# Low halves of ff1's weights made by an accumulating transfer, and q's products one step earlier on VectorE

## The chip, the cores and the metric

The program runs on one core of a Trainium2 chip. Its time is the device time in microseconds (us) of one execution, the median of several. The core's engines work side by side, each through its own list of instructions in order: TensorE (PE, with its weight loads as PEld), VectorE (DVE), ScalarE (ACT), GpSimd (POOL) and SyncE (SP, which here only issues transfers). They wait for each other through semaphores. 16 DMA engines move data between the memory outside the core (HBM) and SBUF.

## The reference, cut to what matters

One layer over 256 tokens of 1024 channels: a token mixer of three groups behind one input projection (1024 to 3072) and one output projection, then an MLP.

```
h = rms_norm(x, norm_mix);  z = h @ w_in                       # 12 column chunks of 256
qs = silu(q);  k = (1 - lb) * sigmoid(-f)                      # HGRN2 group, decays from f
y = concat(rms_norm(griffin), hgrn2, rms_norm(attention));  x = x + y @ w_out
h = rms_norm(x, norm_mlp)
u = square(relu(h @ w_ff1))                                    # 1024 -> 4096
x = x + u @ w_ff2                                              # 4096 -> 1024
return rms_norm(x, norm_final)
```

All data are float32. The products run on TensorE in the type fp32r, which holds fewer bits, so each operand is split into a high part (rounded to fp32r) and a low part (the value less its high part), and each product is the sum of three: high x high, high x low, low x high.

## The kernel before

All weights come in 48 chunks of 1 MB, each a tile of 128 x 2048: 12 of `w_in` (0 to 11), 4 of `w_out` (12 to 15), then `w_ff1[0]`, `w_ff1[1]` (16, 17), and from there `w_ff2` and `w_ff1` by turns: 18 is `w_ff2[0]`, 19 is `w_ff1[2]`, 20 is `w_ff2[1]`, 21 is `w_ff1[3]`, and so on to 45, `w_ff1[15]`, and 46 and 47, the last two of `w_ff2`. SP loads chunk i into one of three `raw` buffers (L94). `split_w` (L96) then makes two halves of it: ACT writes the high half into `wh` (L71, a cast), DVE subtracts it from `raw` into `wl` (L72). When both halves are done, chunk i + 3 is loaded into the buffer that has come free. `wh` and `wl` have four buffers each.

The order of the work is written out by hand. The first 84 slots are groups of TensorE products (input projection, output projection, the first chunk of ff1); a table `plan` says which other steps are issued ahead of each slot. Slot 17 belongs to chunk 4. Ahead of it stands `hg_dqk` (L377), which on TensorE multiplies `qk`, the product of q and k that DVE makes in `hg_q_dve` (L370 to L372). In row 13 of the table the order was: `hg_f_fd` (ACT), the second half of chunk 4's split, `hg_q_dve`.

After the slots a loop runs over the 16 chunks j of `w_ff2`. In each turn TensorE does `ff2_mm` with chunk j (24 products of 512 columns) and then `ff1` for chunk j + 2 (48 products of 256 columns: for each 128 x 128 block, `x1h` and `x1l` with `wh`, `x1h` with `wl`; L301, L302, L303). Between them ACT and DVE split two chunks that come two steps later: one of `w_ff2`, one of `w_ff1`. Then `ff1_out` (L772) takes ff1's result: ACT does the ReLU (`fr`, L778) and its square rounded (`uh`, L779), DVE the exact square and its low part (`fu`, `ul`, L780 and L781). Ahead of the loop stands `x1_ss` (L817), two squares with sums of 128 x 1024 on ACT.

Of the kernel before, what the change touches and what calls it, by code (L numbers as in the profile page):

```python
# [8 lines left out]
F32 = mybir.dt.float32  # L9
F32R = mybir.dt.float32r  # L10
I32 = mybir.dt.int32
AF = mybir.ActivationFunctionType
OP = mybir.AluOpType
AX = mybir.AxisListType

P = 128
S = 256
D = 1024
KT = D // P
# [13 lines left out]
def trunk_kernel(ctx: ExitStack, tc, x, x_t, w_in, w_out, w_ff1, w_ff2, small, hg_norm, norm_final, out):  # L33
    nc = tc.nc
    V, A, G, T = nc.vector, nc.scalar, nc.gpsimd, nc.tensor

    const = ctx.enter_context(tc.tile_pool(name="const", bufs=1))
    RAW = 3
    raw_p = ctx.enter_context(tc.tile_pool(name="raw", bufs=RAW))
    spl_p = ctx.enter_context(tc.tile_pool(name="spl", bufs=4))  # L40
# [20 lines left out]
    def free(name):  # L61
        idle.extend(held.pop(name))

    def wt(name, shape, tag=None, bufs=None, dt=F32):
        return work.tile(shape, dt, name=name, tag=tag or name, bufs=bufs)

    def flat(t):
        return t.rearrange("p a b -> p (a b)")

    def split(hi, lo, src):  # L70
        A.copy(hi, src)  # L71
        V.tensor_tensor(lo, src, hi.bitcast(F32), op=OP.subtract)  # L72
# [4 lines left out]
    NI = len(in_order)  # L77
    IG, IX, IY = 2, 3, 4
    NF = 16
    chunks = [w_in[c] for c, _ in in_order] + [w_out[j] for j in range(4)]  # L80
# [4 lines left out]
            chunks.append(w_ff1[j + 2])  # L85
    NCH = len(chunks)
    raw, hi_w, lo_w = {}, {}, {}

    def load(i, n=1):
        if i < NCH:  # L90
            raw[i] = raw_p.tile([P, 2048], F32, name=f"raw{i}", tag="raw")
            for h in range(n):
                s_ = slice(h * 2048 // n, (h + 1) * 2048 // n)
                nc.sync.dma_start(raw[i][:, s_], chunks[i][:, s_])  # L94

    def split_w(i, h, n=2):  # L96
        if i < NCH:
            if h == 0:
                hi_w[i] = spl_p.tile([P, 2048], F32R, name=f"wh{i}", tag="wh")
                lo_w[i] = spl_p.tile([P, 2048], F32R, name=f"wl{i}", tag="wl")  # L100
            s_ = slice(h * 2048 // n, (h + 1) * 2048 // n)
            split(hi_w[i][:, s_], lo_w[i][:, s_], raw[i][:, s_])
            if h == n - 1:
                load(i + RAW)
# [194 lines left out]
    def mm3(o, l, r, first, last):  # L299
        (lh, ll), (rh, rl) = l, r  # L300
        T.matmul(o, lh, rh, start=first, stop=False)  # L301
        T.matmul(o, lh, rl, start=False, stop=False)  # L302
        T.matmul(o, ll, rh, start=False, stop=last)  # L303
# [27 lines left out]
    yTl = wt("yTl", [P, KT, S], dt=F32R)  # L331
# [399 lines left out]
    x1h = wt("x1h", [P, KT, S], tag="hTh", dt=F32R)  # L731
    x1l = wt("x1l", [P, KT, S], tag="hTl", dt=F32R)
# [29 lines left out]

    FI = NI + 4
    uh, ul = {}, {}

    def ff1_mm(o, i, c, k):
        wh = hi_w[i].rearrange("p (k c) -> p k c", c=CW)
        wl = lo_w[i].rearrange("p (k c) -> p k c", c=CW)
        cs = slice(c * 128, (c + 1) * 128)
        mm3(o, (wh[:, k, cs], wl[:, k, cs]), (x1h[:, k, :], x1l[:, k, :]), k == 0, k == KT - 1)  # L770

    def ff1_evac(j, parts):  # L772
        r = wt("fr", [P, 512], tag="sc", bufs=3)
        u = wt("fu", [P, 512], tag="pr", bufs=2)
        uh[j] = wt("uh", [P, 512], tag="PT", bufs=8, dt=F32R)
        ul[j] = wt("ul", [P, 512], tag="PT", bufs=8, dt=F32R)
        for src, s_ in parts:
            A.activation(r[:, s_], src, AF.Relu)  # L778
            A.activation(uh[j][:, s_], r[:, s_], AF.Square)  # L779
            V.tensor_tensor(u[:, s_], r[:, s_], r[:, s_], op=OP.mult)  # L780
            V.tensor_tensor(ul[j][:, s_], u[:, s_], uh[j][:, s_].bitcast(F32), op=OP.subtract)  # L781
# [3 lines left out]
    def ff1(j, i):  # L785
        ps = ff1_ps[j] = mis(f"f{j}")
        for c in range(2):
            for k in range(KT):
                ff1_mm(ps[:, c * 256:(c + 1) * 256], i, c, k)

    def ff1_out(j):
        ff1_evac(j, [(ff1_ps[j], slice(0, 512))])
        free(f"f{j}")
# [3 lines left out]
    def ff2_mm(j, i, kk, t, n):  # L797
        if j == 0 and kk == 0:
            facc[t, n] = mis(f"fo{t}{n}")
        cs = slice(kk * 256 + t * 128, kk * 256 + (t + 1) * 128)  # L800
        big_mm(facc[t, n], uh[j][:, cs], ul[j][:, cs], i, kk, n, j == 0 and kk == 0,
               (t, n) == (1, 1) and j == NF - 3 and kk == 1)
# [3 lines left out]
    def ff1_first(c, kg):  # L806
        if kg == 0:
            f0[c] = mis(f"f0{c}")[:, 0:256]
        for k in range(4 * kg, 4 * kg + 4):
            ff1_mm(f0[c], FI, c, k)  # L810
# [6 lines left out]
    def x1_ss():  # L817
        for t in range(2):
            A.activation(sq2, xt[:, t, :], AF.Square, accum_out=ss2[:, 0, t:t + 1])
        V.tensor_scalar(ss2[:, 0, :], ss2[:, 0, :], 1.0 / D, EPS, op0=OP.mult, op1=OP.add)  # L820
        V.reciprocal(r2, ss2[:, 0, :])
# [3 lines left out]
    S_ = split_w  # L825
# [16 lines left out]
        10: [(x_bc,), (x_rb,), (hg_f_ev,), (hg_q_ev,), (S_, 3, 0), (S_, 3, 1)],  # L842
        11: [(hg_f_act,), (hg_f_kb,), (S_, 4, 0)],
        12: [(hg_q_act,)],
        13: [(hg_f_fd,), (S_, 4, 1), (hg_q_dve,)],
        14: [(hg_qd,), (S_, 5, 0)],
        15: [(S_, 6, 0)],
        16: [(S_, 6, 1)],
# [56 lines left out]
    S_(FI + 2, 0)  # L905
    S_(FI + 2, 1)
    ff1(1, FI + 1)
    S_(FI + 3, 0)
    S_(FI + 3, 1)
    ff1_out(1)  # L910
    x1_ss()
    nc.sync.dma_start(nfb, bass.AP(tensor=norm_final.tensor, offset=norm_final.offset, ap=[[0, P], [1, D]]))
    i = FI + 2
    tnt = sorted(tn)
    tail = {}
    for j in range(NF):
        if j < NF - 2:
            for kk in range(2):
                for t, n in tnt:
                    ff2_mm(j, i, kk, t, n)  # L920
        else:
            tail[j] = i
        split_w(i + 2, 0)
        split_w(i + 2, 1)
        i += 1
        if j + 2 < NF:
            ff1(j + 2, i)
            split_w(i + 2, 0)
            split_w(i + 2, 1)
            ff1_out(j + 2)  # L930
            i += 1

# [131 lines left out]
```

## Time and profile before

| | before |
|---|---|
| median of 3 runs | 322.01 us (321.96 to 323.01) |
| the profiled execution's own time | 322.01 us |
| its span, first to last instruction | 320.3 us |
| TensorE busy | 309.7 us (97%) |
| VectorE busy | 192.1 us (60%) |
| ScalarE busy | 171.9 us (54%) |
| GpSimd busy | 32.7 us (10%) |
| DMA | 55.71 MB, mean 174 GB/s |

The 1.7 us between the span and the execution's own time lie outside the instructions. Busy shares are means over the whole span; the MLP loop takes the stretch from about 143 us to 302 us. Times below are counted from the start of the span.

### The profile page before, as it was taken

To read this page: it belongs to the slowest core of one execution; us is meant where nothing else is said; L and a number is where in the kernel's file an instruction comes from. 1 tells how busy PE (TensorE), PEld (TensorE's weight loads), DVE (VectorE), ACT (ScalarE), POOL (GpSimd) and SP (SyncE) were. 2 spreads that over 40 slices of the span, in tenths; PEclk is the share of its full clock that TensorE was granted. 3 is DMA by queue.
4 is the path that set the end of the run, shared out by engine and by line. 5 is a ranking of instruction groups with operands and counts; after the bars stand their busy time and mean duration, and the time that the engine had idled before them with its cause. 6 is when DMAs were issued, how large, how long until landed. Compare 5 with 4: busy or idle time off the path is not lost.

```text
span 320.3 us, 5290 instructions
## 1 busy us (share of the span) xinstructions
PE 309.7 (97%) x2164; PEld 283.8 (89%) x2164; DVE 192.1 (60%) x287; ACT 171.9 (54%) x283; POOL 32.7 (10%) x83
## 2 busy tenths in 40 slices
PE   7999899999999999999999999999999999999991
PEld 6999799998999888998899899889989988988881
DVE  1847999994545494598635733753663474375353
ACT  3869499683675370687623642562463265256132
POOL 8338400011502000000000000000000000000000
PEclk9999999999999999999999999999999999999999
DMA  7995463352037336048665256336425624630003
GB/s 198 412 405 209 140 257 131 133 171 93 2 97 298 132 132 264 0 152 327 251 256 217 89 220 263 115 149 262 186 93 249 256 80 191 262 131 3 0 4 129
DMA packets 9961, 55.71 MB, mean 174 GB/s; under 512 B 1232, under 2 KB 1488, under 8 KB 4048
## 3 DMA queue, kind: packets, MB, share of 16 engines
q1 hardware_dynamic: 9216, 54.06, 44.8%
q10 hardware_dynamic: 720, 1.31, 1.3%
q8 instruction: 17, 0.28, 0.3%
q14 instruction: 8, 0.07, 0.1%
HBM read 54.32 MB, written 1.05 MB: 173 GB/s over the span
## 4 chain that ended last, share of the span: by engine, by line
PE 89%; ACT 3%; DVE 2%; DMA 2%; issue 2%; POOLq 0%; POOL 0%; DVEq 0%; ACTq 0%
PE banks L301 27%; PE banks L303 27%; PE banks L302 26%; PE banks L405 2%; DMA raw<-in_w_in_dram 2%; ACT wh L71 1%; PE banks L641 1%; PE banks L659 1%; PE banks L168 1%; PE banks L675 1%; PE banks L676 1%; PE banks L458 1%; PE banks L521 1%; PE banks L674 1%; DVE wl L72 0%
## 5 line engine op out<-in xcount | busy, mean ns | idle before, releaser
L72 DVE TENSOR_TENSOR wl<-raw,wh 128x1024 fp32r<-128x1024 f32 (+1 forms) x100 | 113.6, 1182 | 20.7 <-ACT wh L71 19.0
L71 ACT CAST wh<-raw 128x1024 fp32r<-128x1024 f32 (+1 forms) x100 | 95.4, 1009 | 3.6 <-DMA raw<-in_w_in_dram 3.6
L301 PE MATMUL banks<-x1h,wh 128*128 128x256 f32 x256 | 72.6, 283 | 0.0
L302 PE MATMUL banks<-x1l,wh 128*128 128x256 f32 x256 | 72.5, 283 | 0.0
L303 PE MATMUL banks<-x1h,wl 128*128 128x256 f32 x256 | 72.5, 283 | 0.0
L778 ACT ACTIVATE fr<-banks 128x512 f32<-128x512 f32 (+1 forms) x17 | 9.7, 573 | 87.2 <-PE banks L303 87.2
L780 DVE TENSOR_TENSOR fu<-fr 128x512 f32<-128x512 f32 (+1 forms) x17 | 11.2, 660 | 69.5 <-ACT fr L778 69.5
L303 PE MATMUL banks<-wh,ul 128*128 128x512 f32 (+1 forms) x132 | 51.5, 390 | 0.1
L301 PE MATMUL banks<-wh,uh 128*128 128x512 f32 (+1 forms) x132 | 51.5, 390 | 0.0
L302 PE MATMUL banks<-wl,uh 128*128 128x512 f32 (+1 forms) x132 | 51.5, 390 | 0.0
L301 PEld LDWEIGHTS banks<-x1h,wh 128*128 128x128 f32 x256 | 49.0, 192 | 0.7
L302 PEld LDWEIGHTS banks<-x1l,wh 128*128 128x128 f32 x256 | 49.0, 191 | 0.6
L303 PEld LDWEIGHTS banks<-x1h,wl 128*128 128x128 f32 x256 | 49.1, 192 | 0.0
L301 PE MATMUL banks<-hTh,wh 128*128 128x256 f32 x128 | 37.6, 294 | 0.5 <-ACT hTh L161 0.5
L302 PE MATMUL banks<-hTl,wh 128*128 128x256 f32 x128 | 36.5, 285 | 0.8 <-DVE hTl L162 0.8
L303 PE MATMUL banks<-hTh,wl 128*128 128x256 f32 x128 | 36.3, 284 | 0.0
L303 PEld LDWEIGHTS banks<-wh,ul 128*128 128x128 f32 x132 | 24.9, 189 | 6.1 <-DVE ul L781 0.6
L301 PEld LDWEIGHTS banks<-wh,uh 128*128 128x128 f32 x132 | 25.0, 189 | 5.3 <-ACT uh L779 0.4
L302 PEld LDWEIGHTS banks<-wl,uh 128*128 128x128 f32 x132 | 24.9, 189 | 5.0
L302 PEld LDWEIGHTS banks<-hTl,wh 128*128 128x128 f32 x128 | 24.5, 192 | 1.3 <-DVE hTl L162 1.2
L301 PEld LDWEIGHTS banks<-hTh,wh 128*128 128x128 f32 x128 | 24.5, 191 | 1.2 <-ACT hTh L161 0.7
L303 PEld LDWEIGHTS banks<-hTh,wl 128*128 128x128 f32 x128 | 24.5, 192 | 0.1
(198 smaller groups left out, 412.5 us busy)
## 6 DMA issues: line engine op xcount, KB each, us to landing
raw<-in_w_ff_dram SPq DMA_DIRECT2D x32, 1024.0 KB, 5.0
raw<-in_w_in_dram SPq DMA_DIRECT2D x10, 1024.0 KB, 5.6
raw<-in_w_out_dram SPq DMA_DIRECT2D x4, 1024.0 KB, 4.9
raw<-in_w_in_dram ACTq DMA_DIRECT2D x4, 256.0 KB, 7.3
xtok<-in_x_dram SPq DMA_DIRECT2D x2, 512.0 KB, 7.9
xa<-in_x_dram SPq DMA_DIRECT2D x2, 512.0 KB, 6.7
xa<-in_x_t_dram SPq DMA_DIRECT2D x3, 256.0 KB, 6.2
raw<-in_w_in_dram SPq DMA_DIRECT2D x2, 256.0 KB, 8.1
```

What stands on the lines that cost most here:

```text
L71: A.copy(hi, src)
L72: V.tensor_tensor(lo, src, hi.bitcast(F32), op=OP.subtract)
L168: T.transpose(pair[n % 2][:, i * 256 + t * 128:i * 256 + (t + 1) * 128], src[:, t, (k0 + n) * P:(k0 + n + 1) * P], ident)
L301: T.matmul(o, lh, rh, start=first, stop=False)
L302: T.matmul(o, lh, rl, start=False, stop=False)
L303: T.matmul(o, ll, rh, start=False, stop=last)
L405: T.matmul(ps[:, par, g * 64:(g + 1) * 64], kB[r, hp, hs], rhs, start=True, stop=True)
L458: T.matmul(dst, att_d[:, (hp * 2 + half) * 2 + par, :], bv[:, half, h * 64:h * 64 + 64], start=True, stop=(half == 0))
L521: T.matmul(ps[:, c * 256:(c + 1) * 256], spw[:, wofs + c * 128:wofs + (c + 1) * 128], xc[:, c, :], start=True, stop=True)
L641: T.matmul(ps_s[2 * pair + par][:, os], q[r, c, qs], k[r, c, ks], start=True, stop=True)
L778: A.activation(r[:, s_], src, AF.Relu)
L780: V.tensor_tensor(u[:, s_], r[:, s_], r[:, s_], op=OP.mult)
```

## The change

There are two edits.

First, the 14 chunks `w_ff1[2]` to `w_ff1[15]` (the odd chunk numbers 19 to 45, the set `neg`) are split in another way. ACT writes the negative rounded value, -round(w), into the low tile (two instructions of 128 x 1024) and again into the high tile (two more). Then POOL issues a transfer that reads the same 1 MB chunk from HBM once more and adds it to the low tile in place, so that the low tile holds w - round(w) as before. DVE has no part in it. The high tile is now negative, so the activations it meets are too: `x1_neg` makes `nxh` = -`x1h` and turns `x1l` into -`x1l` (four ACT instructions of 128 x 1024, once, after `ff1_out(1)`). The products are then the same three.

Second, in row 13 of the table `hg_q_dve` goes ahead of `hg_f_fd` and of the second half of chunk 4's split.

```diff
+    neg = set(range(NI + 7, NCH - 2, 2))
...
+    nxh = wt("nxh", [P, KT, S], tag="yTl", dt=F32R)
+
+    def split_n(i):
+        if i in neg:
+            hi_w[i] = spl_p.tile([P, 2048], F32R, name=f"wh{i}", tag="wh")
+            lo_w[i] = spl_p.tile([P, 2048], F32R, name=f"wl{i}", tag="wl")
+            for o in (lo_w[i], hi_w[i]):
+                for s_ in (slice(0, 1024), slice(1024, 2048)):
+                    A.activation(o[:, s_], raw[i][:, s_], AF.Copy, scale=-1.0)
+            nc.gpsimd.dma_start(lo_w[i], chunks[i], accum_op=OP.add)
+            load(i + RAW)
+        else:
+            split_w(i, 0)
+            split_w(i, 1)
+
+    def x1_neg():
+        for s_ in (slice(0, 4), slice(4, 8)):
+            A.activation(flat(nxh[:, s_, :]), flat(x1h[:, s_, :]).bitcast(F32), AF.Copy, scale=-1.0)
+            A.activation(flat(x1l[:, s_, :]), flat(x1l[:, s_, :]).bitcast(F32), AF.Copy, scale=-1.0)
...
-        mm3(o, (wh[:, k, cs], wl[:, k, cs]), (x1h[:, k, :], x1l[:, k, :]), k == 0, k == KT - 1)
+        T.matmul(o, wh[:, k, cs], (nxh if i in neg else x1h)[:, k, :], start=k == 0, stop=False)
+        T.matmul(o, wh[:, k, cs], x1l[:, k, :], start=False, stop=False)
+        T.matmul(o, wl[:, k, cs], x1h[:, k, :], start=False, stop=k == KT - 1)
...
-        13: [(hg_f_fd,), (S_, 4, 1), (hg_q_dve,)],
+        13: [(hg_q_dve,), (hg_f_fd,), (S_, 4, 1)],
...
-    S_(FI + 3, 0)
-    S_(FI + 3, 1)
+    split_n(FI + 3)
     ff1_out(1)
+    x1_neg()
     x1_ss()
...
             ff1(j + 2, i)
-            split_w(i + 2, 0)
-            split_w(i + 2, 1)
+            split_n(i + 2)
             ff1_out(j + 2)
```

On DVE, around chunk 4 of the input projection (`wl_461` and `wl_462` are its low tile, `qc` and `qk` are q's products), before:

```order
L360 TENSOR_SCALAR kB<-kB,omlb 128x256 x2
L72 TENSOR_TENSOR wl_461<-raw_348,wh_460 128x1024 x2
L371 TENSOR_TENSOR qc<-qc,qk 128x512
L372 TENSOR_TENSOR qk<-qc,kB 128x512
L375 TENSOR_TENSOR qd<-qc,fd 128x512
L72 TENSOR_TENSOR wl_511<-raw_368,wh_510 128x1024
```

and in the changed kernel:

```order
L361 TENSOR_SCALAR kB<-kB,omlb 128x256 x2
L72 TENSOR_TENSOR wl_462<-raw_349,wh_461 128x1024
L372 TENSOR_TENSOR qc<-qc,qk 128x512
L373 TENSOR_TENSOR qk<-qc,kB 128x512
L72 TENSOR_TENSOR wl_462<-raw_349,wh_461 128x1024
L376 TENSOR_TENSOR qd<-qc,fd 128x512
L72 TENSOR_TENSOR wl_512<-raw_369,wh_511 128x1024
```

The two products have moved ahead of the second half of chunk 4's low part; `qd` stays behind it.

On ACT, from the split of chunks 18 and 19 to that of chunk 21, at the start of the MLP loop (tiles 1600, 1656, 1701, 1757 are chunks 18 to 21), before:

```order
L71 CAST wh_1600<-raw_1438 128x1024 x2
L71 CAST wh_1656<-raw_1458 128x1024 x2
L778 ACTIVATE fr<-banks 128x512
L779 ACTIVATE uh<-fr 128x512
L819 ACTIVATE sq_208,ss_209<-xa 128x1024 x2
L71 CAST wh_1701<-raw_1574 128x1024 x2
L71 CAST wh_1757<-raw_1606 128x1024 x2
L778 ACTIVATE fr<-banks 128x512
```

and in the changed kernel:

```order
L71 CAST wh_1601<-raw_1439 128x1024 x2
L774 ACTIVATE wl_1658<-raw_1459 128x1024 x2
L774 ACTIVATE wh_1657<-raw_1459 128x1024 x2
L800 ACTIVATE fr<-banks 128x512
L801 ACTIVATE uh<-fr 128x512
L783 ACTIVATE nxh<-x1h 128x1024
L784 ACTIVATE x1l<-x1l 128x1024
L783 ACTIVATE nxh<-x1h 128x1024
L784 ACTIVATE x1l<-x1l 128x1024
L841 ACTIVATE sq_208,ss_209<-xa 128x1024 x2
L71 CAST wh_1707<-raw_1575 128x1024 x2
L774 ACTIVATE wl_1764<-raw_1607 128x1024 x2
```

Eight instructions of 128 x 1024 now stand where two casts stood between chunk 18's split and `x1_ss`. On POOL, whose list had ended here but for the last two powers, 14 transfers have come in; the first three and what stands ahead of them:

```order
L153 TENSOR_TENSOR hrr<-hrv,nhalf 128x8
L153 TENSOR_TENSOR crr<-crv,nhalf 128x2
L775 DMA wl_1658<-in_w_ff_dram 128x2048
L775 DMA wl_1764<-in_w_ff_dram 128x2048
L775 DMA wl_1861<-in_w_ff_dram 128x2048
```

Each waits for ACT's two writes of its low tile. DVE's list has lost 28 subtractions of 128 x 1024.

## Rows read from the trace of the kernel before

**Rows 1.** The page, part 1: busy us (share of the span) and instructions.
```profile
PE 309.7 (97%) x2164; PEld 283.8 (89%) x2164; DVE 192.1 (60%) x287; ACT 171.9 (54%) x283; POOL 32.7 (10%) x83
```

**Rows 2.** PE's waits, two of four: line, waited for: us in total, times, longest.
```profile
PE banks L146 <- POOL ident masks.py:199: 1.4, 1, 1.4
PE banks L380 <- DVE qk L372: 1.2, 1, 1.2
```

**Rows 3.** Timeline of PE at slot 17: start, us, instruction [idle before <-releaser].
```profile
32.95 0.28 PE L302 MATMUL banks<-hTl,wh 128*128 128x256 f32 x1
33.07 0.28 PE L303 MATMUL banks<-hTh,wl 128*128 128x256 f32 x1
34.59 1.10 PE L380 MATMUL banks<-bones,qk 128*128 128x64 f32 x8 [1.24 <-DVE qk L372]
```

**Rows 4.** Timeline of DVE there.
```profile
31.43 1.46 DVE L72 TENSOR_TENSOR wl<-raw,wh 128x1024 fp32r<-128x1024 f32 x1 [1.23 <-ACT wh L71]
32.81 0.99 DVE L371 TENSOR_TENSOR qc<-qc,qk 128x512 f32<-128x512 f32 x1
33.84 0.69 DVE L372 TENSOR_TENSOR qk<-qc,kB 128x512 f32<-128x512 f32 x1
34.45 0.99 DVE L375 TENSOR_TENSOR qd<-qc,fd 128x512 f32<-128x512 f32 x1
```

**Rows 5.** Timeline of ACT there.
```profile
28.85 0.63 ACT L368 ACTIVATE qk<-qc 128x512 f32<-128x512 f32 x1
...
30.37 4.82 ACT L71 CAST wh<-raw 128x1024 fp32r<-128x1024 f32 x5
```

**Rows 6.** Busy time by stretch: us, PE PEld DVE ACT POOL (x), PEclk, DMA share, GB/s.
```profile
245.05:256.40 11.35, 11.35 (x74) 10.26 (x73) 6.02 (x6) 5.02 (x6) 0.00 (x0) 1.00 0.47 186
250.65:256.40 5.75, 5.75 (x49) 5.73 (x48) 1.47 (x2) 0.00 (x0) 0.00 (x0) 1.00 0.92 363
142.80:154.20 11.40, 11.40 (x75) 10.31 (x74) 7.76 (x10) 7.30 (x10) 0.00 (x0) 1.00 0.78 297
32.00:72.00 40.00, 38.74 (x354) 37.02 (x353) 38.73 (x72) 31.71 (x55) 4.40 (x5) 1.00 0.47 166
```

**Rows 7.** Timeline of ACT in one later turn of the loop.
```profile
245.25 0.60 ACT L778 ACTIVATE fr<-banks 128x512 f32<-128x512 f32 x1 [6.31 <-PE banks L303]
...
246.42 3.89 ACT L71 CAST wh<-raw 128x1024 fp32r<-128x1024 f32 x4
```

**Rows 8.** Timeline of PE at the starts of ff1(2), ff1(3) and a later ff1.
```profile
148.43 0.28 PE L301 MATMUL banks<-x1h,wh 128*128 128x256 f32 x1
...
148.66 0.28 PE L303 MATMUL banks<-x1h,wl 128*128 128x256 f32 x1
...
160.02 0.28 PE L303 MATMUL banks<-x1h,wl 128*128 128x256 f32 x1
...
262.26 0.28 PE L303 MATMUL banks<-x1h,wl 128*128 128x256 f32 x1
```

**Rows 9.** Timeline of ACT at the start of the loop.
```profile
137.99 3.88 ACT L71 CAST wh<-raw 128x1024 fp32r<-128x1024 f32 x4
143.01 0.60 ACT L778 ACTIVATE fr<-banks 128x512 f32<-128x512 f32 x1 [1.14 <-PE banks L303]
143.64 0.63 ACT L779 ACTIVATE uh<-fr 128x512 fp32r<-128x512 f32 x1
144.18 1.05 ACT L819 ACTIVATE sq<-xa 128x1024 f32<-128x1024 f32 x1
...
146.40 3.97 ACT L71 CAST wh<-raw 128x1024 fp32r<-128x1024 f32 x4
```

**Rows 10.** The page, part 6: DMA issues, KB each, median us to landing.
```profile
raw<-in_w_ff_dram SPq DMA_DIRECT2D x32, 1024.0 KB, 5.0
```

**Rows 11.** DMA issues from 142 to 159 us, same columns.
```profile
raw<-in_w_ff_dram SPq DMA_DIRECT2D x5, 1024.0 KB, 6.5
```

**Rows 12.** Timeline of SP's issues in that stretch.
```profile
142.06 2.60 SPq L94 DMA_DIRECT2D raw<-in_w_ff_dram  x2
```

## The prediction

> **What bounds the kernel now.** I read the busy shares first: TensorE is busy for 309.7 of 320.3 us [rows 1]. Then its waits: there are four lines of them, and the two longest, 1.4 us for the identity at the very start and 1.2 us for `qk` at L380, are the only ones of over a microsecond [rows 2]. Then the stretches: in a turn of the MLP loop TensorE is busy for all of 11.35 us, beside 6.02 us of DVE, 5.02 us of ACT and a DMA share of 0.47 [rows 6]. So the reader is to see two things. Work taken off DVE in the loop shortens nothing by itself, since nothing there waits for DVE. And the only wait in the middle that the change can take away is that at L380.
>
> **q's products (gain).** TensorE starts its last product ahead of L380 at 33.07, would go on 0.12 later (its step from 32.95 to 33.07), and starts L380 at 34.59 [rows 3]: 34.59 - 33.07 - 0.12 = 1.40 us lost, where the profile's own count is 1.24. `qk` is late because DVE stands idle for 1.23 us from 30.20 until ACT's cast of chunk 4's second half, and only then does that subtraction and `qc` and `qk` [rows 4]. The sigmoid that `qc` needs has ended at 28.85 + 0.63 = 29.48 [rows 5]. In the new order `qc` runs at 30.2 and `qk` ends near 30.2 + 0.8 + 0.69 = 31.7, well ahead of 33.2. The subtraction then starts at about 31.7 and ends near 33.1 (1.46 us), where it had ended at 32.9; its first reader stands about a microsecond behind L380's eight products, so at 34.3: no new wait. `qd` and what follows on DVE come 1.2 to 1.4 us earlier, because the idle time is filled. That matters, since DVE is busy for 38.73 of the 40 us that follow [rows 6]: had only TensorE gained, DVE would take it back. Bounds: 0 (all taken back) and -1.40. I take -1.4, since both engines move together.
>
> **The new split on ACT.** A cast of 128 x 1024 takes 3.88 / 4 = 0.97 us in a row of four [rows 9]; a copy with a scale at this size isn't in the trace, and the nearest is the square, 1.05 [rows 9]. I take 0.97. A turn gets two more, so ACT does 5.0 + 1.9 = 7.0 of 11.35 us: hidden under TensorE. DVE loses 28 subtractions: worth nothing, as above.
>
> **The transfer.** No accumulating transfer and none issued by POOL is in the trace. A plain load of the same 1 MB takes 5.0 us from issue to landing [rows 10]. While loads run, the engines move 363 GB/s [rows 6], so 1 MB is 2.9 us of all of them, and 2.1 us are fixed. An accumulating one must also read the low tile. Its engine time is m x 2.9 us with m between 1 (bytes landed count) and 2 (both reads count, one after the other); by bytes read and written it is three movements for two, m = 1.5, which I take. Where loads stand in SP's queue at the same time, the engines serve both; five loads in the stretch from 142 to 159 take 6.5 us instead of 5.0 [rows 11]. If they alternate, 2.9 us of the other queue's work goes in between: landing = 2.1 + 2.9 x (m + 1) = 7.9, 9.4 or 10.8 us for m = 1, 1.5, 2. Alone and at m = 1 it is 5.0.
>
> The Trainium skill (DMA: Bandwidth & Descriptors, "Issuing engines are not separate DMA queues") says that transfers from SP, ACT and POOL end up on the same 16 engines and interleave; the 6.5 against 5.0 for loads from one queue agrees that engine time is what they share. It speaks against this change: the second read of a chunk is not free because it stands in another queue.
>
> In the steady loop ACT's four instructions start at 246.42 [rows 7], so two casts and the two low writes end at 246.42 + 4 x 0.97 = 250.3; the low part is read in the next ff1 but one turn, at 262.26 [rows 8]. There is room for 12.0 us, and 10.8 fits. Price in the steady loop: 0.
>
> **The start of the loop (loss).** Here there is less room, twice.
> - Chunk 19: ACT's four instructions that start at 137.99 [rows 9] now are chunk 18's casts and 19's low writes, which end at 141.87. The low part is read at 148.66 [rows 8]: room for 6.8 us. Loads are issued at 142.06 and right behind [rows 12], so the engines are shared; the DMA share of that stretch is 0.78 before the change already [rows 6]. Wait: 7.9, 9.4, 10.8 less 6.8 = 1.1, 2.6, 4.0 us; 0 at 5.0.
> - Chunk 21: ACT goes on with 19's two high writes (to 143.8), the ReLU and square (to 145.0), the four of `x1_neg` (to 148.9), `x1_ss` (2.2 us, to 151.1), chunk 20's casts (153.1), and 21's low writes (155.0). Before, these casts had begun at 146.40 + 2 x 0.97. The low part is read at 160.02 plus the first wait: room for 5.0 + 1.1, 2.6, 4.0. Wait: about 1.8 us in all three cases; 0 at 5.0. Load 23 is issued at about 154.5 (20's subtractions), so the engines are shared again.
> - From chunk 23 on ACT is back to its place behind each ReLU, and the room is 9 us and more.
> - `nxh` and the new `x1l`: the first half is done near 147.0, the second at 148.9, needed at 148.43 and 12 products (1.4 us) later: it just fits; at 1.05 us each 0.3 us more, still inside.
>
> The sum, from the profiled execution's own 322.01 (320.3 of span and 1.7 around it, the same as the median): 322.0 - 1.4 + 2.6 + 1.8 = 325.0. With m = 1 it is 322.0 - 1.4 + 1.1 + 1.8 = 323.5; with m = 2, 322.0 - 1.4 + 4.0 + 1.8 = 326.4.
>
> **Rivals.**
> - *Everything lands in time* (not slower): the transfer has the engines nearly to itself and lands in about 5.0 us, both waits are 0, and only the gain is left: 320.6. For it: 5.0 is the median of 32 loads of this size. Against it: in just this stretch loads are back to back. The Trainium skill (same page, "Anatomy of one DMA — SWDGE (gpsimd) path") fits a transfer issued by GpSimd as 2.0 us and its bytes at 436 GB/s, an estimate of 4.4 us here; by that rule this rival is what happens, but no run here shows it, and the fit says nothing of an accumulate. To be faster by over 0.5% it needs a few tenths more from elsewhere, as a shorter step between products with DVE quiet; against that, TensorE does its 48 products in 5.75 us while DVE is busy for only 1.47 of them [rows 6], so DVE's reads don't set that step.
> - *The loop becomes bound by DMA* (much slower): two plain loads take 0.47 x 11.35 = 5.3 us of a turn; with the third the DMA needs 5.3 + 2.9 m. That passes 11.35 at m = 2.1, and from there each of some 12 turns grows: at m = 2.5 by 1.2 us, 14 in all, with about 8 at the start: 322.0 - 1.4 + 8 + 14 = 343; at m = 3 by 2.7 a turn, near 360. For it: no row bounds m from above, and the read of the tile is a second operand that every packet must have. Against it: by bytes alone m stays at 2 or under.
> - *The gain at L380 is taken back* by DVE in the 40 us behind it, the rest as forecast: 326.4. Against it: DVE's idle 1.23 us is filled by the same edit.
>
> **How the numbers follow.** Forecast (waits at chunks 19 and 21 and nowhere else, m from 1 to 2): 0.55, at 325.0, its own range 322.8 to 327. All in time: 0.22. DMA-bound: 0.16. Gain taken back: 0.07. The range 320.4 to 334 leaves out the heavy half of the DMA-bound case and a little below. What a measurement of this kernel can tell from no change is about 0.5%, 1.6 us. Slower than 323.6: most of the forecast, the DMA-bound case and the taken-back one, 0.62. Within 0.5%: the light end of the forecast and most of the case in which all lands in time, 0.30. Faster than 320.4: 0.08.
>
> **What would show it.** Right: L380 starts with no wait and everything on TensorE from there to 142 us stands 1.4 us earlier; TensorE waits for a DMA at the third product of ff1(2) (2.6 us) and of ff1(3) (1.8 us), and nowhere in the later turns, which stay at 11.35 us; POOL's transfers take 8 to 11 us to land at the start. Wrong: no DMA wait on TensorE at all (lands in about 5), or one in every turn with turns longer than 11.4 us (m above 2), or a first product of ff1(2) that waits for ACT's `nxh`.

## The result and the profile after

The changed kernel takes 340.65 us (339.92 to 343.25 in 4 runs) against 322.0 us: a ratio of 1.0589, 95% interval 1.0559 to 1.0618. It is slower by 18.7 us, where 3.0 were forecast, and lies above the range. The profiled execution has a span of 338.2 us and a time of its own of 339.92. Of one run below, e11, two of the four executions, the profiled one among them, ran over 1.5% slower at a lower mean granted clock (0.984 against 0.996), and its time and ratio are those of the other two.

From the page, parts 1, 3 and 6 (busy us and instructions; DMA queue: packets, MB, share of the 16 engines; DMA issues: KB each, median us to landing):

```profile
PE 315.2 (93%) x2164; PEld 287.7 (85%) x2164; DVE 160.2 (47%) x259; ACT 202.2 (60%) x315; POOL 46.3 (14%) x97
...
q1 hardware_dynamic: 9216, 54.06, 44.0%
q0 software_dynamic: 2016, 14.68, 22.0%
...
raw<-in_w_ff_dram SPq DMA_DIRECT2D x32, 1024.0 KB, 6.2
wl<-in_w_ff_dram POOLq DMA_DIRECT2D x14, 1024.0 KB, 12.8
```

Against [rows 1] VectorE has lost 31.9 us and ScalarE has gained 30.3, as the change says, and TensorE's share falls from 97 to 93%: it waits. Queue q0 is the 14 accumulating transfers: 22.0% x 338.2 / 14 = 5.31 us of all 16 engines for each. The prediction read 2.9 us for a plain load from the 363 GB/s of [rows 6]; that row's DMA share is 0.92, so it is 2.9 x 0.92 = 2.7 us. The 14 transfers land in 12.8 us, against 5.0 for the loads of before [rows 10], which now take 6.2 themselves.

TensorE's waits (line, waited for: us in total, times, longest):

```profile
PE banks L792 <- DMA wl<-in_w_ff_dram: 13.1, 7, 6.2
PE banks L147 <- POOL ident masks.py:199: 1.5, 1, 1.5
PE banks L406 <- DVE kB L433: 0.5, 1, 0.5
```

The wait for `qk` of [rows 2] is gone, and the low tile stands first. Timeline of TensorE at q's products and at `ff1(2)`, the places of [rows 3] and [rows 8]:

```profile
33.36 0.28 PE L304 MATMUL banks<-hTh,wl 128*128 128x256 f32 x1
33.48 1.00 PE L381 MATMUL banks<-bones,qk 128*128 128x64 f32 x8
...
147.79 0.28 PE L791 MATMUL banks<-x1l,wh 128*128 128x256 f32 x1
154.29 0.58 PE L792 MATMUL banks<-x1h,wl 128*128 128x256 f32 x1 [6.21 <-DMA wl<-in_w_ff_dram]
154.66 0.42 PE L790 MATMUL banks<-nxh,wh 128*128 128x256 f32 x1
154.88 0.41 PE L791 MATMUL banks<-x1l,wh 128*128 128x256 f32 x1
```

L381 follows the product ahead of it by 0.12 us: no wait. At chunk 19 TensorE stands for 6.2 us, and then its products start 0.22 us apart in place of 0.12. The low tile's two writes and the issue of its transfer stand in the timelines of ACT and POOL:

```profile
139.13 2.01 ACT L774 ACTIVATE wl<-raw 128x1024 fp32r<-128x1024 f32 x2
...
141.46 1.06 POOL L775 DMA_DIRECT2D wl<-in_w_ff_dram  x1 [30.32 <-DVE wl L72]
```

The writes end at 141.14, the issue follows 0.3 us later, and TensorE would have read the tile at 147.79 + 0.12 = 147.91, 6.8 us behind the writes and 6.5 behind the issue.

Busy time of TensorE by stretch (us, PE (x), granted clock, DMA share, GB/s):

```profile
141.40:155.00 13.60, 7.39 (x36) 0.83 0.93 271
154.50:157.00 2.50, 2.50 (x12) 0.50 1.02 370
204.60:208.00 3.40, 3.40 (x18) 0.57 0.87 229
230.00:245.00 15.00, 14.30 (x94) 1.00 0.91 264
245.00:260.00 15.00, 14.88 (x100) 1.00 0.93 251
```

Behind the wait the granted clock is 0.50, the lower level of 1.2 GHz, from 154.5 to 157: 12 products of 256 columns with 0.213 us between starts in place of 0.12, and a slow first step, cost about 1.4 us. The same happens once more behind a step of 2.2 us, of which 2.0 are a wait, that ends at 204.56 (0.57, 16 slow steps, 1.5 us). In the last two stretches it is 1.00, the level of 2.4 GHz. There the DMA share is 0.91 to 0.93, against 0.47 in [rows 6].

To find where the time goes, I compared the start of each TensorE product with the same product of before. It is 1.2 us earlier at 41 us, 0.7 earlier from 42 us on, 7.0 later at 168 us and 17.9 later at the end. So there are two losses: 7.7 us at the start of the MLP loop, and 10.9 us spread over its turns. The steps between products account for them. At the start stand the wait of 6.4 us (the 6.2 shown, and the rest of a step) and 1.4 us of low clock, 7.8; later seven waits of 0.3 to 2.2 us, counted in the same way, 8.2 in all, 1.5 us of low clock, 0.6 us in the slow first steps behind the other waits, and a wait of 0.7 for DVE's `ul` at 322 us, together 11.0. The later waits come in about every second turn: where no wait went before, there are 11.7 us from the issue to the read, and behind a wait of a microsecond the next transfer has that microsecond more.

### The profile page after: what moved, and what is told of

Same layout as the page of the kernel before. It is cut to its first block, busy times and chain, and to the rows that moved or that the text cites. A ratio compares the mean times of both kernels' runs of the same rounds, so it can differ in the third digit from the quotient of the medians.

```text
span 338.2 us, 5313 instructions
## 1 busy us (share of the span) xinstructions
PE 315.2 (93%) x2164; PEld 287.7 (85%) x2164; DVE 160.2 (47%) x259; ACT 202.2 (60%) x315; POOL 46.3 (14%) x97
## 3 DMA queue, kind: packets, MB, share of 16 engines
HBM read 69.00 MB, written 1.05 MB: 207 GB/s over the span
## 4 chain that ended last, share of the span: by engine, by line
PE 58%; DMA 29%; DVE 5%; ACT 4%; issue 2%; SPq 0%; POOLq 0%; POOL 0%; DVEq 0%; ACTq 0%
DMA wl<-in_w_ff_dram 23%; PE banks L302 11%; PE banks L303 10%; PE banks L304 10%; PE banks L792 7%; PE banks L791 6%; PE banks L790 6%; DMA raw<-in_w_in_dram 5%; DVE wl L72 2%; PE banks L406 2%; ACT wh L71 2%; PE banks L642 1%; PE banks L660 1%; PE banks L169 1%; ACT wl L774 1%
## 5 line engine op out<-in xcount | busy, mean ns | idle before, releaser
L72 DVE TENSOR_TENSOR wl<-raw,wh 128x1024 fp32r<-128x1024 f32 (+1 forms) x72 | 81.8, 1167 | 19.6 <-ACT wh L71 18.0
L792 PE MATMUL banks<-x1h,wl 128*128 128x256 f32 x256 | 74.8, 292 | 13.3 <-DMA wl<-in_w_ff_dram 13.1
L71 ACT CAST wh<-raw 128x1024 fp32r<-128x1024 f32 (+1 forms) x72 | 68.7, 995 | 4.0 <-DMA raw<-in_w_in_dram 4.0
L790 PE MATMUL banks<-nxh,wh 128*128 128x256 f32 x224 | 64.5, 288 | 0.0
L792 PEld LDWEIGHTS banks<-x1h,wl 128*128 128x128 f32 x256 | 50.3, 196 | 14.9 <-DMA wl<-in_w_ff_dram 14.9
L791 PEld LDWEIGHTS banks<-x1l,wh 128*128 128x128 f32 x256 | 50.2, 196 | 0.6
L790 PEld LDWEIGHTS banks<-nxh,wh 128*128 128x128 f32 x224 | 44.3, 198 | 0.6
L775 POOL DMA_DIRECT2D wl<-in_w_ff_dram x14 | 12.4, 886 | 179.5 <-PE banks L303 116.5
L774 ACT ACTIVATE wl<-raw 128x1024 fp32r<-128x1024 f32 x28 | 28.0, 1049 | 0.0
L774 ACT ACTIVATE wh<-raw 128x1024 fp32r<-128x1024 f32 x28 | 27.8, 1040 | 0.0
## 6 DMA issues: line engine op xcount, KB each, us to landing
wl<-in_w_ff_dram POOLq DMA_DIRECT2D x14, 1024.0 KB, 12.8
```

The source lines that it names most:

```text
L774: A.activation(o[:, s_], raw[i][:, s_], AF.Copy, scale=-1.0)
L775: nc.gpsimd.dma_start(lo_w[i], chunks[i], accum_op=OP.add)
L790: T.matmul(o, wh[:, k, cs], (nxh if i in neg else x1h)[:, k, :], start=k == 0, stop=False)
L791: T.matmul(o, wh[:, k, cs], x1l[:, k, :], start=False, stop=False)
L792: T.matmul(o, wl[:, k, cs], x1h[:, k, :], start=False, stop=k == KT - 1)
```

## The experiments

Each kernel ran beside the kernel before on the same chip; ratios are to that.

**The parts of the change.** Run e1 is before with the new order of q alone.

```diff
-        13: [(hg_f_fd,), (S_, 4, 1), (hg_q_dve,)],
+        13: [(hg_q_dve,), (hg_f_fd,), (S_, 4, 1)],
```

> The kernel before with only the second edit (q's products ahead of the second half of chunk 4's low part). Both theories of the loss say that it lies in the transfers, so this one is not slower than before. In the changed kernel TensorE stood 1.2 us earlier behind L380 and kept 0.7 us of it: I expect 320.6 to 321.3 us (0.2 to 0.4% faster), no wait at L380, and perhaps a new one of 0.5 us at the next product with kB.

Measured: 320.7 us, ratio 0.9952 (0.9931 to 0.9972). No version is faster (e3 below can't be told from it), and the gain at q's products (L380 starts at 32.96 instead of 34.59) is kept to the end. All of TensorE's waits of it that the profile lists stand in the first 10 us:

```profile
PE banks L146 <- POOL ident masks.py:199: 1.4, 1, 1.4
PE banks L302 <- DVE hTl L162: 0.8, 2, 0.4
```

Run e2 is the changed kernel with the old order of row 13 (the edit above, undone).

> The changed kernel without the second edit: the accumulating transfers alone. If the two edits are independent, its time is that of the changed kernel plus what the second edit is worth, 340.7 + 0.7 to 1.4 = 341.4 to 342.1 us. If the earlier start of the loop collides with the transfers, it is not slower than the changed kernel.

Measured: 342.94 us, ratio 1.0625 (1.0579 to 1.0670), 0.8 us above what was expected, which lies inside the interval. The wait for `qk` is back:

```profile
PE banks L381 <- DVE qk L373: 1.6, 1, 1.6
```

The loss is all in the new split.

Run e3 keeps the negative high part, `nxh` and the negated `x1l`, but VectorE adds `raw` to the negative high part; there is no transfer.

```diff
-            for o in (lo_w[i], hi_w[i]):
...
-                    A.activation(o[:, s_], raw[i][:, s_], AF.Copy, scale=-1.0)
-            nc.gpsimd.dma_start(lo_w[i], chunks[i], accum_op=OP.add)
+                    A.activation(hi_w[i][:, s_], raw[i][:, s_], AF.Copy, scale=-1.0)
+                    V.tensor_tensor(lo_w[i][:, s_], raw[i][:, s_], hi_w[i][:, s_].bitcast(F32), op=OP.add)
```

> All of the change but the transfers: the high part of the 14 chunks is written negative by ACT, x1_neg is there, and the low part is made by DVE, which adds raw to the negative high part. Theory 1 (the transfers' engine time is the loss): 320.6 to 322 us, no wait of TensorE in the loop. Theory 3 (ACT's negations and the new operand nxh are the loss): it stays above 330 us, or keeps the wait at the first product of ff1(2).

Measured: 320.96 us, ratio 0.9959 (0.9940 to 0.9979), as e1. So the negation costs nothing that can be measured, and neither did VectorE's subtractions: with them (here, as additions) or without (e8 below, 320.89 us), the time is the same. The 19.7 us between this run and the changed kernel are the transfer and the two writes that it needs of ScalarE; e8 has these writes too, so they cost nothing by themselves.

**What one transfer takes.** Run e4 copies the chunk in place of adding it.

```diff
-            nc.gpsimd.dma_start(lo_w[i], chunks[i], accum_op=OP.add)
+            nc.gpsimd.dma_start(lo_w[i], chunks[i])
```

> The changed kernel with a plain copy from POOL in place of the accumulating one: same issue, same bytes from HBM, same waits, but the low tile isn't read back (it then holds the whole weight and not the low part). Theory 1 (a read-modify-write takes 1.84 times a load's engine time and fills the DMA): engine time falls from 5.3 to about 2.9 us a transfer, DMA share in a turn from 0.93 to about 0.72, landing to about 8 us, waits only at chunks 19 and 21 of 1 to 2 us: 322 to 324 us. Theory 2 (a transfer issued by POOL is late by itself): it lands after 12 us or more and the time stays at 337 us or more.

Measured: 327.51 us, ratio 1.0159 (1.0122 to 1.0195). Its queue's share, its issues and TensorE's waits, and the stretch behind the one wait (columns as above):

```profile
q0 software_dynamic: 2016, 14.68, 11.3%
...
wl<-in_w_ff_dram POOLq DMA_DIRECT2D x14, 1024.0 KB, 7.9
```

```profile
PE banks L792 <- DMA wl<-in_w_ff_dram: 4.3, 1, 4.3
```

```profile
147.00:152.00 5.00, 0.71 (x4) 0.74 0.82 336
152.00:158.00 6.00, 6.00 (x36) 0.65 0.71 251
```

A copy takes 11.3% x 325.8 / 14 = 2.63 us of the engines and lands in 7.9 (10.9 at chunk 19, its longest). No later turn waits. So the accumulate doubles the engine time, and in this order of transfers it is what makes the later turns late. The time is above the 322 to 324 us expected: at chunk 19 the copy is 4.3 us late and not 1 to 2, and at chunk 21 it is in time. Here too the wait is followed by a low granted clock, and 20 slow products cost 1.9 us.

Run e7 accumulates from the high tile in SBUF, so HBM is not read a second time (the low tile's value is another).

```diff
-            nc.gpsimd.dma_start(lo_w[i], chunks[i], accum_op=OP.add)
+            nc.gpsimd.dma_start(lo_w[i], hi_w[i].bitcast(F32), accum_op=OP.add)
```

> The changed kernel with the accumulating transfer's source taken from the chunk's high tile in SBUF and not from HBM; the low parts then hold twice the negative high part. If the engine time of 5.3 us is that of the read-modify-write, it stays and the time stays at 337 to 343 us. If it is the second read of HBM, the engine time falls to 3 us or less and the time to 328 us or less.

Measured: 349.16 us, ratio 1.0835 (1.0779 to 1.0891), with

```profile
q0 software_dynamic: 2016, 14.68, 20.5%
...
wl<-wh POOLq DMA_DIRECT2D x14, 1024.0 KB, 12.1
```

That is 20.5% x 346.2 / 14 = 5.07 us each. So the second read of HBM isn't what makes it long; what is left is the accumulation into the destination. The time is longer than the 337 to 343 us expected, because the transfer now reads the high tile and is issued only when that is written too: 2.2 us behind the low tile's writes instead of 0.3, with as much less room. By packets of 8 KB, the median is 0.628 us for an accumulating one and 0.325 for one of the plain copy.

Run e8 leaves each transfer in but lets it add into a spare float32 tile that nobody reads; the low tiles keep the negative high part.

```diff
-            nc.gpsimd.dma_start(lo_w[i], chunks[i], accum_op=OP.add)
+            nc.gpsimd.dma_start(scr, chunks[i], accum_op=OP.add)
...
+    scr = wt("scr", [P, 2048], tag="yTh")
+    G.memset(scr, 0.0)
```

> The changed kernel with the 14 accumulating transfers going into a spare float32 tile that nothing reads; the low tiles keep the negative high part. They then wait only for each other and run one behind the other from about 135 us on. No type conversion is in them: if the conversion to fp32r is part of the 5.3 us, engine time falls well below it; I expect 5.3. TensorE can wait only for loads that come late. If the loss is the low tile's landing, it has no waits of over 1 us at the places of before: 321 to 325 us. If plain contention of the loads were enough, it is 330 us or more.

Measured: 320.89 us, ratio 0.9966 (0.9950 to 0.9981), as e3. Queue, issues and stretches of the loop (columns as above):

```profile
q0 software_dynamic: 2016, 14.68, 24.0%
...
raw<-in_w_ff_dram SPq DMA_DIRECT2D x32, 1024.0 KB, 7.9
scr<-in_w_ff_dram POOLq DMA_DIRECT2D x14, 1024.0 KB, 10.8
```

```profile
155.00:170.00 15.00, 15.00 (x91) 1.00 1.01 316
230.00:245.00 15.00, 15.00 (x98) 1.00 1.01 291
```

The engines are full, the loads land in 7.9 us instead of 5.0, and TensorE never waits in the loop. Each transfer takes 24.0% x 318.6 / 14 = 5.46 us of the engines, so the type fp32r of the low tile isn't what makes it long either. So the traffic costs nothing by itself: the loads have that much room. What costs is the deadline of the low tile.

**Start and later turns apart.** Run e5 gives the transfer to the later 12 chunks (23 to 45) only; 19 and 21 are made by VectorE as in e3. Run e6 gives it to every other one of these (23, 27 and so on to 43).

```diff
+    acc = set(range(NI + 11, NCH - 2, 2))   # e5; e6: step 4
...
+            if i in acc:
...
+                nc.gpsimd.dma_start(lo_w[i], chunks[i], accum_op=OP.add)
+            else:
...
```

> The changed kernel with chunks 19 and 21 made as in the run with DVE's addition, so that accumulating transfers begin with chunk 23 (12 of them). The two tight places at the start of the loop are gone. Theory 1a (the DMA is the bound of every turn: 5.4 us of loads and 5.3 of the accumulate in 11.36, and a transfer lands about 12.8 us after its issue where there is room for 12.0): waits of 0.5 to 1.5 us in half or more of the turns, 326 to 331 us. Theory 1b (the later waits are an echo of the first long one and of the backlog it left): no waits, 320.7 to 322 us.

> As the run with 12 transfers, but only every second ff1 chunk from 23 on (6 transfers); the others get their low part from DVE's addition. Over two turns the DMA then needs 2 x 5.4 + 5.3 = 16.1 of 22.7 us, a share of 0.71. Theory 1a: a transfer shares the engines with at most two loads and lands in 8 to 11 us, inside the room of 12: no waits, 320.5 to 321.5 us. Theory 2 (each accumulating transfer is slow by itself, 12.8 us whatever else runs): waits of about 1 us at each of the six, 325 us or more.

Measured: e5 332.74 us, ratio 1.0324 (1.0290 to 1.0358); e6 330.97 us, ratio 1.0252 (1.0212 to 1.0291). TensorE's waits, the issues and the loop's stretch (columns as above) of e5, then of e6:

```profile
PE banks L798 <- DMA wl<-in_w_ff_dram: 10.5, 9, 1.5
```

```profile
wl<-in_w_ff_dram POOLq DMA_DIRECT2D x12, 1024.0 KB, 13.5
...
160.00:300.00 140.00, 129.55 (x813) 1.00 0.91 255
```

```profile
PE banks L798 <- DMA wl<-in_w_ff_dram: 8.0, 6, 2.3
```

```profile
wl<-in_w_ff_dram POOLq DMA_DIRECT2D x6, 1024.0 KB, 12.9
...
155.00:300.00 145.00, 136.95 (x855) 0.99 0.71 221
```

The later turns lose 332.74 - 320.96 = 11.8 us on their own, so their loss is no echo of the long wait at the start; that start costs 340.65 - 332.74 = 7.9, which is the wait (6.4 with the step of a product that it replaces) and the slow products behind it (1.4). In e6 every transfer stands alone among its neighbours, the mean DMA share from 155 to 300 us is 0.71, and still all six are late, so theory 1a falls; theory 2 (each transfer is slow by itself) forecast this, and e9 below decides on it. The packets of one of its transfers tell more: issued at 182.30, it finds a load whose packets go on until 186.6; its first packet starts 3.8 us after the issue; it has the engines to itself for about a microsecond; then the next load's packets come in between, one for one; the last ends 13.8 us after the issue.

**Is it the order?** Run e9 (12 chunks) and e10 (all 14) write the low tile and issue the transfer ahead of the `w_ff2` chunk's casts, so that no load is ahead of it.

```diff
+    def split_pair(a, b):
...
+        for s_ in halves:
+            A.activation(lo_w[b][:, s_], raw[b][:, s_], AF.Copy, scale=-1.0)
+        nc.gpsimd.dma_start(lo_w[b], chunks[b], accum_op=OP.add)
+        for s_ in halves:
+            split(hi_w[a][:, s_], lo_w[a][:, s_], raw[a][:, s_])
+        load(a + RAW)
...
```

> The run with 12 transfers (from chunk 23 on), with ACT writing the negative value into the low tile ahead of the w_ff2 chunk's casts and not behind them, and the transfer issued right there: the same 12 transfers and the same bytes, issued 1.9 us earlier and ahead of the turn's first load. Theory 4 (each transfer lands about 12.8 us after its issue because it starts behind a load in flight, moves at half a load's pace and takes turns with the next load; the room is 12.0): room becomes 13.9, the first packet comes 1.5 to 2 us after the issue and not 3.8, landing 9 to 11 us, and no wait in the loop: 320.5 to 321.5 us. Theory 1a (the DMA's whole capacity is the bound): the share stays at 0.93 or more of a turn and waits go on, 328 us or more.

> The same order with all 14 transfers, so the two tight places at the start are back. Chunk 19's low writes end at about 138.6 us on the changed kernel's clock, room 8.7 us, landing 9 to 12: a wait of 1 to 3 us there (6.4 in the changed kernel) with some slow clock behind it; chunk 21's room is 6.9 us plus that wait, so another of 1 to 3 us. None later. 323.5 to 327 us by theory 4; by theory 1a 335 us or more.

Measured: e9 339.36 us, ratio 1.0538 (1.0517 to 1.0560); e10 344.63 us, ratio 1.0699 (1.0678 to 1.0719). In e9 the transfer lands in 8.6 us, as hoped, so it isn't slow by itself: theory 2 falls. In the medians of the packets the first starts 1.6 us after the issue, against 3.8 in the changed kernel, and 6.4 us lie between the first and the end of the last, against 8.3, since little of a load now comes in between. But ScalarE now waits for `raw` (ScalarE's waits, then the issues):

```profile
ACT wl L798 <- DMA raw<-in_w_ff_dram: 70.0, 12, 6.8
```

```profile
raw<-in_w_ff_dram SPq DMA_DIRECT2D x32, 1024.0 KB, 7.5
wl<-in_w_ff_dram POOLq DMA_DIRECT2D x12, 1024.0 KB, 8.6
```

The `w_ff1` chunk's load must now have landed before the `w_ff2` chunk can be cast, and that cast and subtraction set free the buffer for the next load. This ring takes 12.9 us from issue to issue, and TensorE, whose turn is 11.4, follows it. The test moved the loads as well as the transfer, and so it shows how fast a transfer lands without its neighbours, but not what the time would then be.

Run e11 (12 chunks) and e12 (14) hold the load behind the transfer back instead: ScalarE issues it after `ff1_out`. In e12 the 512 KB of `norm_final` are also loaded near the end of the loop and not at its start.

```diff
-            load(i + RAW)
...
+            nc.scalar.dma_start(raw[i], chunks[i])
```

> The run with 12 transfers, in its own order, but the second load of each turn (the w_ff2 chunk three ahead, not needed for another 17 us) is issued by ACT behind ff1_out and so after the transfer has landed, where it had been issued 1.6 us behind the transfer. Nothing is removed: the DMA moves the same 3 MB a turn. Theory 5 (the order on the engines, not their capacity: the transfer starts behind the first load and then takes turns with the second one): it lands in 9 to 10.5 us and not in 13.5, inside the room of 11.6, and the loop has no waits: 320.5 to 322 us. Theory 1a (capacity): the held load now delays the next turn's first load, whose room is 9.7 us, and waits of about a microsecond go on in other places: 328 us or more.

> The same with all 14 transfers, and norm_final's 512 KB loaded near the end of the loop and not at its start. At chunk 19 the transfer still starts behind load 21, so it lands 9 to 10 us after its issue where there is room for 6.4: a wait of 2.5 to 3.5 us (6.4 in the changed kernel), with perhaps a microsecond of slower clock behind it; at chunk 21 a wait of 0 to 2 us; none later by theory 5: 324 to 327 us. By theory 1a 333 us or more.

Measured: e11 326.67 us, ratio 1.0139 (1.0118 to 1.0160); e12 339.76 us, ratio 1.0560 (1.0526 to 1.0594). Neither lies in what one of the theories expects for e11; e12 lies where capacity puts it, with a wait of 7.5 us at chunk 19. In e11's profile waits are left in 4 turns, 6.8 us in all, and the transfer lands in 11.8 us. ScalarE's place comes only about 6.6 us after the transfer's issue, so the held load still cuts into its end: the order was changed by half.

In e13 (12 chunks) and e14 (14) GpSimd issues that load itself, right behind the transfer in the same queue.

```diff
-            load(i + RAW)
...
+            (nc.gpsimd if i - RAW in acc else nc.sync).dma_start(raw[i], chunks[i])
```

> The later 12 transfers only (chunks 23 to 45; 19 and 21 are split by VectorE as in the run with the new order of q alone), and the load that is freed by each of these splits is issued by GpSimd right behind the transfer, so that it stands behind it in the same queue and can't take turns with it. Theory 5 (the loop's loss is the order of the transfers: the accumulate waits for the load ahead of it and then takes turns with the load behind it): the transfer starts some 3.8 us after its issue and then needs 5.3 us with little beside it, plus its tail: it lands in 9.5 to 10.5 us, inside the room of 11.6 us; TensorE waits for a low tile in no turn or by tenths, 320.5 to 322.5. The freed load lands some 3 us later than now, about 8 to 10 us after its split, which ScalarE's next casts have room for. Rival (capacity: 0.92 of the 16 engines' time is taken, so the tile is late in whatever order): waits of 0.5 to 1.5 us stay in most turns, 326 to 333.

> All 14 transfers, each with the freed load behind it in GpSimd's queue. Theory 5: no waits in the later turns, but chunk 19's stays, shorter than now because nothing takes turns with the transfer: landing 9.5 to 10.5 against room 6.8, a wait of 3 to 4 us and up to 2 us of lower granted clock behind it, 325 to 327. Rival (capacity): 6 us at chunk 19 and about a microsecond in each of most later turns, 336 to 341.

Measured: e13 324.33 us, ratio 1.0063 (1.0039 to 1.0087); e14 332.03 us, ratio 1.0289 (1.0268 to 1.0311). TensorE's waits and the issues of e13, its stretch in the loop, then TensorE's waits of e14 and its stretch behind the wait at chunk 19:

```profile
PE banks L802 <- DMA wl<-in_w_ff_dram: 3.0, 6, 0.9
```

```profile
wl<-in_w_ff_dram POOLq DMA_DIRECT2D x12, 1024.0 KB, 12.1
raw<-in_w_ff_dram POOLq DMA_DIRECT2D x11, 1024.0 KB, 12.6
```

```profile
160.00:300.00 140.00, 137.02 (x859) 1.00 0.95 262
```

```profile
PE banks L802 <- DMA wl<-in_w_ff_dram: 9.4, 5, 5.8
...
153.00:158.50 5.50, 5.50 (x27) 0.50 0.93 302
```

Of the later turns' 11.8 us, 332.74 - 324.33 = 8.4 go by this order alone, with the DMA share at 0.95 where it was 0.91 in e5, so the engines' capacity is not what bounds the loop; the whole kernel gains 340.65 - 332.03 = 8.6 by it. Neither theory is right to the last microsecond. The expected landing of 9.5 to 10.5 us was not met: it is 12.1, 0.4 us past the room of 11.7, and waits of up to a microsecond are left. In the packets of the transfer issued at 169.76 111 of 128 have ended by 180.4, and the load behind it has begun, but the last one ends at 182.1, and only then, at 182.5, can TensorE go on. What made these last ones late I have not separated. The packets show a second reason. The moved load no longer cuts into its own transfer, but it takes turns with the load that stands ahead of the next one, which is in flight for 9.0 us (median) where it was 7.1 in e5. So half of a transfer's packets have ended no earlier than in e5, 8.1 us after the issue against 7.9; nine tenths have, 10.1 against 11.0. Only the order behind the transfer has become better. In e14 TensorE still waits 5.8 us at chunk 19 and then runs 27 slow products (2.5 us): with 6.8 us of room the tile is late in either order.

## Why the prediction was wrong

- **What bounds the kernel, and VectorE's work:** right. The 28 subtractions were worth nothing; e3 has them as additions and is as fast as e1.
- **q's products:** right, -1.4 forecast, and in e1 -1.6 at the line (0.2 of it stood already at the product ahead, so -1.4 is the wait) and 320.7 - 322.0 = -1.3 in the whole; VectorE did not take it back there. In the profiled execution of the changed kernel 0.5 us of it went again at 42 us, to a wait for `kB`. e3, e5 and e8 run the same instructions up to the loop, and their profiles don't have it, so it belongs to the execution and not to the change.
- **The split on ScalarE:** the price was right. A write of 128 x 1024 took 1.05 us with its neighbour's start 0.95 behind, and all of it is hidden, as are `nxh` and `x1l` (e8).
- **The transfer's engine time:** under. m was taken as 1.5, with bounds of 1 and 2; measured 5.31 us, 5.31 / 2.9 = 1.84. The 2.9 itself was read too high, since its row's DMA share is 0.92; by the 2.63 us of the plain copy (e4) m is 2.0, the upper bound: both reads count.
- **The landing:** this is the step that failed. The sum took 9.4 us. The formula "landing = 2.1 + 2.9 x (m + 1)" gives 10.3 us at m = 1.84, and 10.8 at its upper end; measured 12.8. It counts one load that alternates with the transfer, but there are two: the one ahead, for which the first packet starts 3.8 us after the issue instead of the 1.6 of e9 (2.2 us), and the one behind, which takes turns. 10.3 + 2.2 = 12.5. That the transfers of several queues interleave on the same engines was weighed in the prediction with the Trainium skill (DMA: Bandwidth & Descriptors, "Issuing engines are not separate DMA queues"). The packets of e6 agree for the load behind the transfer; the one ahead of it, issued 0.7 us earlier, goes first. The prediction counted one neighbour only. The Trainium skill's fit (same page, "Anatomy of one DMA — SWDGE (gpsimd) path"), by which the estimate was 4.4 us, is not met by any run here, where loads are always near: the shortest copy took 7.7 us (e4), the shortest accumulate 8.1 (e8's first, with nothing ahead of it).
- **"Price in the steady loop: 0":** this follows from that step, and is most of the error. Room 12.0 us, as forecast, less the 0.3 from ScalarE's last write to the issue is 11.7, the landing 12.8, and so the waits of about a microsecond: 11.8 us by e5. I had compared 12.0 with an upper end of 10.8 and called it safe. A margin of a tenth doesn't cover a term that was left out.
- **Chunk 19:** the place and the room (6.8) were right, the wait was 6.4 instead of 2.6, again by the landing. The clock was not in the sum: the slow products behind the wait cost another 1.4 us, which no term held. **Chunk 21:** no wait. It was 1.8 "in all three cases" because the first wait was added to the room in each; behind a wait of 6.4, with slow products and with low writes that ended 1.0 us earlier than forecast (154.0), there were 12.8 us from the issue to the read, and the transfer landed in 12.3.
- **The rivals:** "Everything lands in time" fell (e4, where even a copy is late at chunk 19). "The loop becomes bound by DMA" named the sign seen, longer turns with a DMA wait, and at m = 2.5 a time of 343, but not the cause: two loads and the transfer need 5.3 + 5.3 = 10.6 us of a turn's 11.35, so m is under its threshold of 2.1, and e8 runs the same traffic at a DMA share of 1.01 at no cost. "The gain at L380 is taken back" did not happen in e1. What bounded the loop was not the amount of traffic but the place of one transfer in it.

The sum as it should have stood: 322.0 - 1.4 + 0.5 + 6.4 + 1.4 + 11.8 = 340.7. That it meets 340.65 so closely is in part luck: 11.8 is of e5, where the changed kernel's own profile has 10.9 for the later turns, and the 0.5 is of one execution.

## What to carry to other kernels

A transfer with a deadline is to be priced by its place in the queues: what is in flight when it is issued, and what is issued behind it before it lands, each add their packets; the room must cover these and its own. If it must be issued, put the loads that have time behind it in its own queue (8.4 us of 11.8 came back here). And before an engine is relieved with a DMA, look whether anything waits for that engine: here nothing did, so the new order of q alone (320.7 us) has the whole gain.

## What the runs showed of the hardware

- An accumulating transfer took 5.1 to 5.5 us of the 16 engines for 1 MB, a plain one 2.6; from HBM or from SBUF, into fp32r or float32 (5.31 in the changed kernel, 5.07 in e7, 5.46 in e8; 2.63 in e4).
- GpSimd's transfer starts its first packet 1.6 us after the issue where nothing is ahead (e9), and 3.8 us with a load issued 0.7 us before it (e6). In the packets of e6 that load goes first, to its end at 4.3 us, and a load issued behind the transfer takes turns with it, one packet (0.324 us) for one (0.628).
- After the steps of 4.4 to 8.4 us at chunk 19 (the changed kernel, e2, e4, e7, e12, e14), and after some of 2.2 to 2.8 us (the changed kernel, e6, e7), TensorE was granted the lower level (0.50), and 12 to 27 products ran with starts 0.213 us apart in place of 0.12. That costs 1.1 to 2.5 us more, and stands in no list of waits. The nine of 0.9 to 1.7 us of e5 were followed by none of it, and neither were the two of 2.1 and 2.2 in e10 and the one of 2.0 in e7.
- A loop whose DMA share is 1.0 need not be slower (e8: 320.89 us).
